# Splitting the first 8 MB load of a streaming ReLU-sum into a 2 MB and a 6 MB load

## The chip, the core and the metric

The kernel runs on one core of one Trainium2 chip. The metric is the device time of one execution in microseconds (us). The core has four engines that matter here: VectorE (DVE), ScalarE (ACT), GpSimd (POOL) and SyncE (SP), whose queue issues every DMA of this kernel; TensorE (PE) runs only a few matrix products whose result nobody reads. Sixteen DMA engines carry the data between the main memory (HBM) and the on-chip memory (SBUF), which has 128 partitions.

## The reference

The input `x` is 32 x 512 x 1024 float32, which is 16,384 rows of 1024 numbers, 67.1 MB. For each row the kernel clamps at zero and adds up:

```
relu_x = np.maximum(x, 0)
return np.sum(relu_x, axis=-1).astype(np.float32)
```

The output is 32 x 512 float32, 64 KB. So every byte of the input is read once, one maximum and one addition are done on each number, and almost nothing is written.

## The kernel before

**Tiling.** With 128 partitions there are NT = 128 rows for each partition. Rows are counted per partition by `m`, from 0 to 127, and `ROWS` = 16 of them make one full load: 128 partitions x 16 rows x 4 KB = 8 MB. Three SBUF buffers (`NBUF` = 3, called `io`) of that size are used in turn. The loads are:

- `j` = 0 to 6, the loop over `TWO`, `ACT` and `DVE`: seven full loads of 8 MB.
- then `TAIL`: one load of 8 rows a partition (4 MB) and one of 4 rows (2 MB), and the last 4 rows in four smaller loads of 1151, 436.5, 259 and 201.5 KB.

That is 13 loads. All are issued by SP through `load` (L104), in this order, on one queue, and each has a semaphore of its own.

**Where the rows lie.** The first 8 MB of the input (`xf`, L84) are one contiguous stretch: partition p holds 16 consecutive rows, so that the stretches of neighbouring partitions are 64 KB apart. The remaining 56 MB (`xv`, L85) are cut the same way with 112 rows a partition, so that there the pitch is 448 KB, and each full load takes 64 KB out of each. The functions `rows` and `sums` give the source of a load and the target of a store for a row number `m`.

**What is done to a load.** For each number n in `TWO[j]`, ACT clamps n rows a partition in one instruction (`clamp`, L145) and then DVE adds each row up in one instruction (`total`, L153), which waits for that ACT instruction. Load 0 and load 1 are one such piece of 16 rows, loads 2 to 4 two pieces of 8, load 5 two pieces of 7 and two rows that ACT does alone (`act_row`, L160), and load 6 is done row by row, 8 by ACT and 8 by DVE (`dve_row`, L168). The very first ACT instruction is the loading of the ReLU table (L143), and it waits for load 0.

**What sets the order around the change.** Load j, for j of 3 and up, goes into the buffer of load j - 3, so its issue on SP waits on the DVE semaphore until DVE has finished with that buffer (`freed[j - NBUF]`). Loads 0, 1 and 2 wait for nothing. `open_without_barrier` moves the first load alone (`EARLY` = 1) ahead of the program's opening. The stores come behind all loads in SP's order: the sums of the first 16 rows (`store(0, ROWS, ...)`, 8 KB, 64 bytes a partition), then 110 rows (55 KB), then the last two (1 KB), which waits for the last instructions of ACT and DVE. At the end SP waits until all stores have landed (L52).

Of the kernel before, what the change touches and what calls it, by code (L numbers as in the profile page):

```python
# [7 lines left out]
P = 128  # L8

ROWS = 16  # L10
NBUF = 3


TWO = [[16], [16], [8, 8], [8, 8], [8, 8], [7, 7], []]
ACT = [0, 0, 0, 0, 0, 2, 8]
DVE = [0, 0, 0, 0, 0, 0, 8]

# [2 lines left out]
TAIL = [8, 4]  # L20
# [11 lines left out]
def kernel(tc: tile.TileContext, x: bass.AP, out: bass.AP):  # L32
    nc = tc.nc
    sems = Semaphores(tc)

    tc.close()
    tc.compile()
    nc.cur_bb = nc.bb_map[tc.start_bb_name]
    body = nc.cur_bb.bb.instructions
    ends = list(body)  # L40
    body.clear()
    n_stores = relu_sum(nc, sems, x, out)
    body.extend(ends)


    nc.cur_bb = nc.bb_map[tc.start_bb_name + "_end"]
    nc.cur_bb.bb.instructions.clear()
    nums = sorted(s.num for s in (*sems.loads, sems.act, sems.dve))
    cleared = range(nums[0], nums[-1] + 1)
    assert len(cleared) == len(nums)  # L50
    nc.sync.sem_clear(cleared)
    nc.sync.wait_ge(sems.stored, 16 * n_stores).then_inc(sems.stored, -16 * n_stores)  # L52
    open_without_barrier(tc, EARLY)


class Semaphores:
    def __init__(self, tc: tile.TileContext):
        n = len(TWO) + len(TAIL) + 4
        self.loads = [tc.alloc_semaphore(f"load{i}") for i in range(n)]
        self.act = tc.alloc_semaphore("act")  # L60
        self.dve = tc.alloc_semaphore("dve")
        self.end = self.loads[-1]
        self.stored = tc.alloc_semaphore("stored")


def relu_sum(nc, sems: Semaphores, x: bass.AP, out: bass.AP):
    x_flat = x.flatten_outer_dims()
    N, D = x_flat.shape
    NT = N // P
    NB = len(TWO)  # L70
    assert N == P * NT == P * ROWS * (NB + 1)
    assert sum(TAIL) == ROWS - 4
    assert HEAD + MIDDLE + LAST_DVE == D and HEAD == 2 + LAST_DVE

    bufs = [nc.alloc_sbuf_tensor(f"io{i}", [P, ROWS, D], F32) for i in range(NBUF)]
    res = nc.alloc_sbuf_tensor("res", [P, NT], F32)
# [3 lines left out]
    last = nc.alloc_sbuf_tensor("last", [P, 2 + n_last + 2], F32)  # L80


    N1 = P * ROWS
    xf = x_flat[:N1].rearrange("(p m) d -> p m d", p=P)  # L84
    xv = x_flat[N1:].rearrange("(p m) d -> p m d", p=P)  # L85
    o_flat = out.rearrange("b s -> (b s)")
    of = o_flat[:N1].rearrange("(p m) -> p m", p=P)
    ov = o_flat[N1:].rearrange("(p m) -> p m", p=P)

    def rows(m, n):  # L90
        if m < ROWS:
            return xf[:, m : m + n, :]
        return xv[:, m - ROWS : m - ROWS + n, :]

    def sums(m, n):
        if m < ROWS:
            return of[:, m : m + n], res[:, m : m + n]
        return ov[:, m - ROWS : m - ROWS + n], res[:, m : m + n]

    n_load = n_act = n_dve = n_store = 0  # L100

    def load(dst, src, after=None):
        nonlocal n_load
        dma = nc.sync.dma_start(out=dst, in_=src)  # L104
        if after:
            dma.wait_op(sems.dve, after[1], "sem-ge")
        dma.then_inc(sems.loads[n_load], 16)
        n_load += 1
        return sems.loads[n_load - 1]

    def store(m, n, act, sem, count):
        nonlocal n_store
        dst, src = sums(m, n)
        if act:
            nc.sync.wait_ge(sems.act, act)
        nc.sync.dma_start(out=dst, in_=src).wait_op(sem, count, "sem-ge").then_inc(
            sems.stored, 16
        )
        n_store += 1
# [20 lines left out]
    def clamp(ap, loaded):  # L140
        nonlocal n_act
        if n_act == 0:
            nc.scalar.preload_act_table(RELU).wait_op(loaded, 16, "sem-ge")  # L143
            loaded = None
        i = nc.scalar.activation(out=ap, in_=ap, func=RELU)  # L145
        if loaded is not None:
            i.wait_op(loaded, 16, "sem-ge")
        i.then_inc(sems.act, 1)
        n_act += 1

    def total(ap, m, n):
        nonlocal n_dve
        nc.vector.tensor_reduce(  # L153
            out=res[:, m : m + n], in_=ap, axis=mybir.AxisListType.X, op=ADD
        ).wait_op(sems.act, n_act, "sem-ge").then_inc(sems.dve, 1)
        n_dve += 1

    def act_row(ap, accum_out, loaded):
        nonlocal n_act
        i = nc.scalar.activation(out=ap, in_=ap, func=RELU, accum_out=accum_out)  # L160
        if loaded is not None:
            i.wait_op(loaded, 16, "sem-ge")
        i.then_inc(sems.act, 1)
        n_act += 1

    def dve_row(ap, accum_out, loaded):
        nonlocal n_dve
        i = nc.vector.tensor_scalar(  # L168
            out=ap,
            in0=ap,  # L170
            scalar1=0.0,
            scalar2=None,
            op0=MAX,
            op1=ADD,
            accum_out=accum_out,
        )
        if loaded is not None:
            i.wait_op(loaded, 16, "sem-ge")
        i.then_inc(sems.dve, 1)
        n_dve += 1  # L180

    def multiply(done):
        ps = nc.alloc_psum_tensor("ps", [P, MM_COLS], F32)
        rows_of = bufs[(NB - 2) % NBUF]
        for k in range(N_MM):
            i = nc.tensor.matmul(  # L186
                ps[:, :], rows_of[:, 0, :P], rows_of[:, 1, :MM_COLS], start=True, stop=True
            )
            if k == 0:
                i.wait_op(sems.dve, done, "sem-ge").then_inc(sems.end, 1)  # L190

    freed = []
    m = 0
    for j in range(NB):
        buf = bufs[j % NBUF]
        loaded = load(buf[:, :, :], rows(m, ROWS), j >= NBUF and freed[j - NBUF])
        c = 0
        act_waits = dve_waits = loaded
        for n in TWO[j]:
            clamp(buf[:, c : c + n, :], act_waits)  # L200
            total(buf[:, c : c + n, :], m + c, n)
            act_waits = None
            c += n
        for _ in range(ACT[j]):
            act_row(buf[:, c, :], res[:, m + c : m + c + 1], act_waits)
            act_waits = None
            c += 1
        for _ in range(DVE[j]):
            dve_row(buf[:, c, :], res[:, m + c : m + c + 1], dve_waits)
            dve_waits = None  # L210
            c += 1
        assert c == ROWS
        freed.append((n_act, n_dve))
        m += ROWS


    multiply(freed[-1][1])
    buf = bufs[NB % NBUF]
    c = 0
    for n in TAIL:  # L220
        loaded = load(
            buf[:, c : c + n, :], rows(m, n), None if c else freed[NB - NBUF]
        )
        for i in range(n):
            if i % 2 == 0 or (n == 8 and i == 7):
                act_row(buf[:, c, :], res[:, m : m + 1], loaded if i == 0 else None)
            else:
                dve_row(buf[:, c, :], res[:, m : m + 1], loaded if i == 1 else None)
            c += 1
            m += 1  # L230

    flat = buf[:, :, :].rearrange("p c d -> p (c d)")
    src = rows(m, 4).rearrange("p c d -> p (c d)")
    at = c * D
    head = 2 * D + HEAD
# [4 lines left out]
    loaded = load(flat[:, at : at + head], src[:, :head])  # L240
# [8 lines left out]
    for lo, hi, n, first, second in (  # L249
# [3 lines left out]
        loaded = load(flat[:, at + lo : at + hi], src[:, lo:hi])  # L253
        act_part(flat[:, at + lo : at + lo + n], last[:, first : first + 1], (loaded, 16))
        dve_part(flat[:, at + lo + n : at + hi], last[:, second : second + 1], (loaded, 16))
    loaded = load(last[:, 2 : 2 + n_last], src[:, middle:end])
# [1 line left out]

    store(0, ROWS, freed[0][0], sems.dve, freed[0][1])
    store(ROWS, NT - ROWS - 2, sums_act, sems.dve, sums_dve)


# [62 lines left out]
```

## Time and profile before

| what | value |
|---|---|
| three timed runs | 160.92, 160.82 and 160.94 us, median 160.92 |
| span of the profiled execution, first to last instruction | 159.9 us |
| what lies around the span, if the profiled execution took the median time | about 1.0 us |
| data read | 67.11 MB, 420 GB/s over the span |
| DVE busy | 118.7 us (74%) |
| ACT busy | 103.6 us (65%) |
| PE busy | 8.6 us |
| load 0 issued, first consumer starts | 0.00 us, 22.27 us |
| last store issued, landed | 158.51 us, 1.4 us later |

The profile gives the profiled execution's span, and no time of its own besides; the third row is the difference of the median and the span. The page counts an engine as busy only while it works on an instruction. DMA queues are told in packets: one packet is what one DMA engine moves in one piece, here the stretch of one partition. In the views that follow, "idle before, releaser" is the time an engine stood still ahead of an instruction and the thing whose end let it go on; `SPq` is SyncE's queue, which issues DMAs and is otherwise idle.

### The profile page before, as it was taken

The numbers are of one execution on the slowest core, as the hardware profiler recorded it, in microseconds if no ns is written. First come the engines' busy times: TensorE is split into PE (matmuls) and PEld (weight loads), VectorE is DVE, ScalarE is ACT, GpSimd is POOL, SyncE is SP. The second block draws the span as 40 slices with busy tenths as digits, with TensorE's granted clock in tenths as the row PEclk, the third lists the DMA queues.
The fourth block names the chain that finished last, engine by engine and source line by source line (L and its number), as shares of the span: only waits on it lengthen the run. The fifth ranks groups of instructions, "written<-read, shape, count | busy, mean of one in ns | idle before, by whom it ended". The sixth has DMA issues, their size and how long they took to land.

```text
span 159.9 us, 157 instructions
## 1 busy us (share of the span) xinstructions
PE 8.6 (5%) x16; PEld 3.6 (2%) x16; DVE 118.7 (74%) x44; ACT 103.6 (65%) x53; POOL 1.0 (1%) x5
## 2 busy tenths in 40 slices
PE   0000000000000000000000000000000000000695
PEld 0000000000000000000000000000000000000241
DVE  0000000006999799999999999999999799999986
ACT  0000049993599807997099950999429993397995
POOL 0000000000000000000000000000000000000001
DMA  8996996996996997999979979969969969899993
GB/s 279 508 492 295 524 492 295 524 492 295 525 492 295 524 475 311 524 393 393 525 328 459 508 344 459 508 295 508 492 295 524 492 295 524 377 402 402 428 396 110
DMA packets 2304, 67.18 MB, mean 420 GB/s; under 512 B 640, under 2 KB 768, under 8 KB 1024
## 3 DMA queue, kind: packets, MB, share of 16 engines
q1 hardware_dynamic: 2304, 67.18, 97.8%
HBM read 67.11 MB, written 0.07 MB: 420 GB/s over the span
## 4 chain that ended last, share of the span: by engine, by line
DMA 45%; DVE 45%; ACT 9%; SPq 1%; issue 0%
DMA io<-in_x_dram 45%; DVE res L153 43%; ACT io L145 9%; DVE io L168 1%; SPq L104 1%; DVE io L127 1%; DVE io L266 0%
## 5 line engine op out<-in xcount | busy, mean ns | idle before, releaser
L153 DVE TENSOR_REDUCE res<-io 128x8 f32<-128x8192 f32 (+2 forms) x10 | 101.1, 10173 | 39.2 <-ACT io L145 39.2
L145 ACT ACTIVATE io<-io 128x8192 f32<-128x8192 f32 (+2 forms) x10 | 81.8, 8218 | 25.9 <-DMA io<-in_x_dram 25.9
L160 ACT ACTIVATE io<-io 128x1024 f32<-128x1024 f32 x18 | 18.8, 1042 | 6.6 <-DMA io<-in_x_dram 6.6
L186 PE MATMUL ps<-io 128*128 128x512 f32 x16 | 8.6, 698 | 149.5 <-DVE io L168 149.5
L168 DVE TENSOR_SCALAR_CACHE_REDUCE io<-io 128x1024 f32<-128x1024 f32 x14 | 16.2, 1215 | 0.5 <-DMA io<-in_x_dram 0.4
L143 ACT ACT_TABLE_LOAD x1 | 1.3, 1283 | 22.3 <-DMA io<-in_x_dram 22.3
L186 PEld LDWEIGHTS ps<-io 128*128 128x128 f32 x16 | 3.6, 231 | 153.7 <-DVE io L168 149.5
L160 ACT ACTIVATION_READ_ACCUMULATOR io<-io 128x1 f32 x18 | 3.3, 186 | 0.0
L246 POOL TENSOR_SCALAR io<-io 128x254 f32<-128x254 f32 x1 | 0.8, 841 | 155.4 <-DMA io<-in_x_dram 155.4
L168 DVE DVE_READ_ACCUMULATOR io<-io 128x1 f32 x14 | 1.2, 82 | 0.0
L127 DVE TENSOR_SCALAR_CACHE_REDUCE io<-io 128x552 f32<-128x552 f32 (+1 forms) x2 | 1.1, 594 | 0.0
L122 ACT ACTIVATE io<-io 128x321 f32<-128x321 f32 (+1 forms) x2 | 0.9, 426 | 0.1
L266 DVE SCALAR_TENSOR_TENSOR io<-last,io 128x254 f32<-128x254 f32 x1 | 0.4, 423 | 0.0
L122 ACT ACTIVATION_READ_ACCUMULATOR io<-io 128x1 f32 x2 | 0.4, 186 | 0.0
L122 ACT ACTIVATE last<-last 128x153 f32<-128x153 f32 x1 | 0.3, 330 | 0.0
L122 ACT ACTIVATION_READ_ACCUMULATOR last<-last 128x1 f32 x1 | 0.2, 187 | 0.0
L127 DVE DVE_READ_ACCUMULATOR io<-io 128x1 f32 x2 | 0.2, 82 | 0.0
L311 POOL MEMSET const-uint8-127<- 128x1 uint8 x1 | 0.1, 102 | 0.0
L311 POOL MEMSET const-bfloat16-1.0<- 128x1 bf16 x1 | 0.1, 101 | 0.0
L311 POOL MEMSET const-float32-0.0<- 128x1 f32 x1 | 0.1, 99 | 0.2 <-issue 0.2
L311 POOL MEMSET const-float32-1.0<- 128x1 f32 x1 | 0.1, 98 | 0.0
L266 DVE DVE_READ_ACCUMULATOR io<-last,io 128x1 f32 x1 | 0.1, 82 | 0.0
## 6 DMA issues: line engine op xcount, KB each, us to landing
io<-in_x_dram SPq DMA_DIRECT2D x1, 4096.0 KB, 23.7
io<-in_x_dram SPq DMA_DIRECT2D x1, 2048.0 KB, 28.3
io<-in_x_dram SPq DMA_DIRECT2D x1, 1151.0 KB, 30.6
io<-in_x_dram SPq DMA_DIRECT2D x1, 436.5 KB, 31.2
io<-in_x_dram SPq DMA_DIRECT2D x1, 259.0 KB, 31.4
last<-in_x_dram SPq DMA_DIRECT2D x1, 201.5 KB, 31.4
io<-in_x_dram SPq DMA_DIRECT2D x7, 29.0
out_dram<-res SPq DMA_DIRECT2D x1, 55.0 KB, 1.6
```

The source lines that it names most:

```text
L104: dma = nc.sync.dma_start(out=dst, in_=src)
L122: nc.scalar.activation(out=ap, in_=ap, func=RELU, accum_out=accum_out).wait_op(*after, "sem-ge").then_inc(sems.end, 1)
L127: i = nc.vector.tensor_scalar(out=ap, in0=ap, scalar1=0.0, scalar2=None, op0=MAX, op1=ADD, accum_out=accum_out,)
L143: nc.scalar.preload_act_table(RELU).wait_op(loaded, 16, "sem-ge")
L145: i = nc.scalar.activation(out=ap, in_=ap, func=RELU)
L153: nc.vector.tensor_reduce(out=res[:, m : m + n], in_=ap, axis=mybir.AxisListType.X, op=ADD).wait_op(sems.act, n_act, "sem-ge").then_inc(se ...
L160: i = nc.scalar.activation(out=ap, in_=ap, func=RELU, accum_out=accum_out)
L168: i = nc.vector.tensor_scalar(out=ap, in0=ap, scalar1=0.0, scalar2=None, op0=MAX, op1=ADD, accum_out=accum_out,)
L186: i = nc.tensor.matmul(ps[:, :], rows_of[:, 0, :P], rows_of[:, 1, :MM_COLS], start=True, stop=True)
L246: nc.gpsimd.tensor_scalar(out=clamped, in0=clamped, scalar1=0.0, scalar2=None, op0=MAX).wait_op(loaded, 16, "sem-ge").then_inc(sems.end, 1)
L266: nc.vector.scalar_tensor_tensor(out=clamped, in0=last[:, : 2 + LAST_DVE], scalar=0.0, in1=clamped, op0=MAX, op1=ADD, accum_out=res[:, NT ...
L311: nc = _bacc.Bacc("TRN2", target_bir_lowering=False, num_devices=1)
```

## The change

The first 8 MB are no longer one contiguous stretch cut into 128 pieces of 16 rows. They become two stretches. The first 2 MB hold 4 rows a partition (`FIRST` = 4; stretches 16 KB apart), the next 6 MB hold 12 rows a partition (48 KB apart). Each is loaded by a DMA of its own into its part of the same buffer, so there are 14 loads. `EARLY` stays 1, so the 2 MB load alone is moved ahead of the opening. ACT and DVE take this buffer in a piece of 4 rows and a piece of 12 rows; the ACT instruction of each piece waits for its own load (the table load for the first). Load 3 waits for both pieces as it did for the one. The sums of these rows leave in two stores, of 16 and 48 bytes a partition, where there was one of 64. All other rows keep their places, loads and instructions.

```diff
-TWO = [[16], [16], [8, 8], [8, 8], [8, 8], [7, 7], []]
+FIRST = 4
+TWO = [[FIRST, ROWS - FIRST], [16], [8, 8], [8, 8], [8, 8], [7, 7], []]
...
-        n = len(TWO) + len(TAIL) + 4
+        n = len(TWO) + len(TAIL) + 5
...
-    N1 = P * ROWS
-    xf = x_flat[:N1].rearrange("(p m) d -> p m d", p=P)
-    xv = x_flat[N1:].rearrange("(p m) d -> p m d", p=P)
...
+    parts = []
+    for lo, hi in ((0, FIRST), (FIRST, ROWS), (ROWS, NT)):
+        src = x_flat[P * lo : P * hi].rearrange("(p m) d -> p m d", p=P)
+        dst = o_flat[P * lo : P * hi].rearrange("(p m) -> p m", p=P)
+        parts.append((lo, hi, src, dst))
...
-        loaded = load(buf[:, :, :], rows(m, ROWS), j >= NBUF and freed[j - NBUF])
+        if j == 0:
+            loads = [
+                load(buf[:, lo:hi, :], rows(lo, hi - lo)) for lo, hi, _, _ in parts[:2]
+            ]
+        else:
+            loads = [
+                load(buf[:, :, :], rows(m, ROWS), j >= NBUF and freed[j - NBUF])
+            ]
         c = 0
-        act_waits = dve_waits = loaded
-        for n in TWO[j]:
+        act_waits = dve_waits = loads[0]
+        for k, n in enumerate(TWO[j]):
+            if k and k < len(loads):
+                act_waits = loads[k]
             clamp(buf[:, c : c + n, :], act_waits)
             total(buf[:, c : c + n, :], m + c, n)
...
-    store(0, ROWS, freed[0][0], sems.dve, freed[0][1])
+    store(0, FIRST, freed[0][0], sems.dve, freed[0][1])
+    store(FIRST, ROWS - FIRST, 0, sems.dve, freed[0][1])
     store(ROWS, NT - ROWS - 2, sums_act, sems.dve, sums_dve)
```

More of the change, by code (lines that the diff above doesn't have):

```diff
@@ L80, in relu_sum, with part_of @@
     last = nc.alloc_sbuf_tensor("last", [P, 2 + n_last + 2], F32)
-    N1 = P * ROWS
-    xf = x_flat[:N1].rearrange("(p m) d -> p m d", p=P)
-    xv = x_flat[N1:].rearrange("(p m) d -> p m d", p=P)
     o_flat = out.rearrange("b s -> (b s)")
-    of = o_flat[:N1].rearrange("(p m) -> p m", p=P)
-    ov = o_flat[N1:].rearrange("(p m) -> p m", p=P)
+    parts = []
[3 more added lines that the diff above has]
+        parts.append((lo, hi, src, dst))
+    def part_of(m, n):
+        return next(p for p in parts if p[0] <= m and m + n <= p[1])
     def rows(m, n):
-        if m < ROWS:
-            return xf[:, m : m + n, :]
-        return xv[:, m - ROWS : m - ROWS + n, :]
+        lo, _, src, _ = part_of(m, n)
+        return src[:, m - lo : m - lo + n, :]
     def sums(m, n):
-        if m < ROWS:
-            return of[:, m : m + n], res[:, m : m + n]
-        return ov[:, m - ROWS : m - ROWS + n], res[:, m : m + n]
+        lo, _, _, dst = part_of(m, n)
+        return dst[:, m - lo : m - lo + n], res[:, m : m + n]
     n_load = n_act = n_dve = n_store = 0
```

## The prediction

> **What bounds the kernel now.** I read the page's slices and queue first, then the table of stretches cut at the arrivals of the loads, then the order of instructions, and last the waits of SP's queue against the chain. The page:
>
> ```profile
> span 159.9 us, 157 instructions
> ...
> DMA  8996996996996997999979979969969969899993
> ...
> q1 hardware_dynamic: 2304, 67.18, 97.8%
> HBM read 67.11 MB, written 0.07 MB: 420 GB/s over the span
> ## 4 chain that ended last, share of the span: by engine, by line
> DMA 45%; DVE 45%; ACT 9%; SPq 1%; issue 0%
> ```
>
> The queue's packets fill 97.8% of what sixteen engines have to give in the span. The chain at the bottom looks different: it gives DVE as much as the DMA. Which is right is decided by the arrivals. Stretches cut where ACT gets each full load (columns: stretch and length, busy time of the engines, TensorE clock, DMA share, GB/s):
>
> ```profile
> 22.30:41.60 19.30, 0.00 (x0) 0.00 (x0) 4.15 (x1) 15.11 (x3) 0.00 (x0) 1.00 1.00 435
> 41.60:60.95 19.35, 0.00 (x0) 0.00 (x0) 18.53 (x2) 13.86 (x2) 0.00 (x0) 1.00 1.00 434
> 60.95:80.30 19.35, 0.00 (x0) 0.00 (x0) 19.35 (x2) 13.96 (x3) 0.00 (x0) 1.00 1.00 434
> 99.65:119.00 19.35, 0.00 (x0) 0.00 (x0) 19.35 (x3) 13.96 (x3) 0.00 (x0) 1.00 1.00 434
> ```
>
> Every 8 MB takes the same 19.35 us with a DMA share of 1.00, whether DVE was busy for 4 us of it or for all of it. Had a load waited for a free buffer, its arrival would be late; none is. The order of work around the first buffer:
>
> ```profile
> 22.27 1.28 ACT L143 ACT_TABLE_LOAD   x1 [22.27 <-DMA io<-in_x_dram]
> 23.56 13.86 ACT L145 ACTIVATE io<-io 128x16384 f32<-128x16384 f32 x1
> 37.45 17.22 DVE L153 TENSOR_REDUCE res<-io 128x16 f32<-128x16384 f32 x1 [37.45 <-ACT io L145]
> 41.60 13.86 ACT L145 ACTIVATE io<-io 128x16384 f32<-128x16384 f32 x1 [4.18 <-DMA io<-in_x_dram]
> 54.70 0.33 SPq L104 DMA_DIRECT2D io<-in_x_dram  x1
> 55.49 17.22 DVE L153 TENSOR_REDUCE res<-io 128x16 f32<-128x16384 f32 x1 [0.82 <-ACT io L145]
> 60.95 7.03 ACT L145 ACTIVATE io<-io 128x8192 f32<-128x8192 f32 x1 [5.49 <-DMA io<-in_x_dram]
> ```
>
> DVE frees buffer 0 and SP issues load 3 at 54.70, but load 2 keeps the DMA engines until 60.95: the issue is 6.25 us early. SP's later issues, at 72.73, 89.92, 107.11 and 124.29, precede the arrivals at 80.29, 99.65, 118.99 and 138.35 of the loads ahead of them by 7 to 14 us. So this wait of the queue, large as it is, costs nothing:
>
> ```profile
> SPq L104 <- DVE res L153: 121.6, 5, 53.3
> ```
>
> The kernel is bound by the DMA stream from its first packet to its last, plus a beginning and an end in which the stream does not run. The beginning and the end:
>
> ```profile
> 0.00:0.90 0.90, 0.00 (x0) 0.00 (x0) 0.00 (x0) 0.00 (x0) 0.19 (x4) 1.00 0.00 0
> 1.60:1.90 0.30, 0.00 (x0) 0.00 (x0) 0.00 (x0) 0.00 (x0) 0.00 (x0) 1.00 1.33 437
> ...
> 157.60:157.80 0.20, 0.20 (x2) 0.00 (x0) 0.20 (x3) 0.20 (x1) 0.00 (x0) 1.00 0.02 2
> 158.20:158.40 0.20, 0.00 (x0) 0.00 (x0) 0.20 (x2) 0.20 (x2) 0.00 (x0) 1.00 0.00 0
> 158.40:159.20 0.80, 0.00 (x0) 0.00 (x0) 0.08 (x2) 0.07 (x1) 0.00 (x0) 1.00 0.00 0
> ```
>
> A packet counts in the stretch in which it starts. No packet starts in the first 0.90 us, and the last of the sixteen engines starts only between 1.60 and 1.90. At the end DMA is idle around 157.7 and from 158.2 to 159.2, before the last store.
>
> **The change, part by part.** The sum is made on the profiled execution: span 159.94 us, and about 0.98 around it to the median of 160.92 (the runs lie within 0.12 of each other). I call the change visible from 0.2%, that is 0.32 us: below 160.60 or above 161.24.
>
> *Two loads for one, in the stream.* The trace's packet records give, per packet and engine, 2.418 us for 64 KB, 1.213 for 32 KB and 0.611 for 16 KB (the later full loads, the 4 MB and the 2 MB load). Doubling the size adds 0.602 for 16 KB and 1.205 for 32 KB, so 16 KB cost 0.602 and each packet 0.009 besides; 48 KB is then 1.815. Each engine serves 8 partitions: before 8 x 2.418 = 19.344, after 8 x (0.611 + 1.815) = 19.408, so +0.064, and a completion packet of 0.009 more: +0.073 on the path, because nothing in the stream hides it. The timeline agrees: ACT gets load 6 at 138.35 and the 4 MB load at 148.06, 9.71 after, against half of 19.35 = 9.68; a load more in a full queue costs a few hundredths.
>
> The Trainium skill, page "SBUF — State Buffer", section "The DMA setup-cost knee", speaks against this change: every transfer pays roughly 2 us that do not scale with its bytes, so one should coalesce into the largest single transfer. Were that paid in series, the sum would be 160.92 + 2.0 = 162.9 as an estimate from that page; the 9.71 above shows no such term for a load that is queued behind another, so the trace contradicts it there, and shows it only at the beginning of the stream.
>
> *The seam.* The 6 MB load has to be queued when the 2 MB load runs out. SP issued its first three loads at 0.00, 0.43 and 0.91, and the first packet started 1.01 after the first issue. Issued at 0.43, the 6 MB load is ready at about 1.5 to 2.3 (the last engine's start was 0.83 behind the first's). The 2 MB load ends 8 x 0.611 = 4.89 after the engines' start and their first delay, at 5.9 at the earliest. Cover: over 3.5 us. Cost taken: 0; if the cover were gone, up to 1.4, the time from issue to landing of the lone last store.
>
> *The start.* The first packets take 2.63 to 3.38 us in the records where the later ones take 2.42, and the engines start over 0.83 us. As all move the same bytes afterwards, they keep this order: sixteen completions of load 0 arrive from 21.27 to 22.25, fourteen by 21.75 and the two last at 22.12 and 22.25; the same tail is in every later load up to the end. So the slowest engine's start sets the end of the kernel. The change alters the first addresses and the size of the first packet (16 KB), and no row shows that. From below: if the two late engines joined the other fourteen, 0.50 is won. From above: a further delay of the same 0.50. The delay looks like a latency, which 16 KB pay as 64 KB do, and the pitch of 448 KB of later loads runs at the full rate as 64 KB does, so I take 0.
>
> *Instructions of ACT and DVE.* The table load and the first clamp move forward: the 2 MB load lands at 22.27 - (19.344 - 4.888) = 7.8 instead of 22.27. ACT: 1.28 + 4/16 x 13.86 = 4.7, to 12.5; DVE 4/16 x 17.22 = 4.3, to 16.9. The 12 rows land at 22.35: ACT 10.4 to 32.8, DVE 12.9 to 45.7. The two extra instructions cost ACT and DVE some tenths at most, in the 4.18 us that ACT idles ahead of 41.60. Load 3 can be issued at 45.7 instead of 54.70, but DMA engines have loads 1 and 2 until 61: hidden, 0. From load 1 on (ACT at 41.60 + 0.07, DVE behind it) nothing moves but by the 0.07.
>
> *Issues on SP.* One load more, 0.43 us, past which loads 1 and 2 move from 0.43 and 0.91 to 0.9 and 1.4; they are needed at 22 and 41. One store more at 127.2, about 0.37; behind it SP next waits for ACT until 156.9, so it is hidden.
>
> *The stores in the ring.* The 8 KB store is issued at 127.21 and lands 31.0 us later, since it queues behind the loads. Its packets (64 B, 0.011 us) become twice as many (16 and 48 B; the 8 B packets of the last store take 0.007 to 0.009), which adds 8 x 0.010 + 0.009 = 0.09 per engine, after the last load, in the hole at 157.7. If the hole is too small, the 55 KB store shifts by under 0.1, and behind it stands the idle time of 1.0 ahead of the last store's packets. Nothing on the path: 0.
>
> Sum: +0.064 + 0.009 = +0.073: the span becomes 160.0, and the time 160.92 + 0.07 = 161.0.
>
> **The rivals.**
> - *The late engines start better.* The two late ones lose part of their 0.50: 160.6 to 160.9, and at the full amount 161.0 - 0.50 = 160.5. For it: a first packet of 16 KB keeps sixteen engines closer together in memory. Against it: nothing shows that addresses set the delay.
> - *The late engines start worse*, by the same 0.25 to 0.50: 161.25 to 161.5. For it: a third and fourth load are issued while the engines start. Against it: that was so with three.
> - *The seam opens* (the slower side): the 6 MB load's packets come after the 2 MB load ran out, or the engines restart there. Price up to 1.4, so 161.3 to 162.4; it decides from a gap of 0.25 us. Against it: 3.5 us of cover, and the seams of the tail show 0.03. For it: those seams had full queues for 20 us, this one lies in the first 6 us.
> - *Earlier work pays* (the chain is right and the DMA waits for DVE): load 3 is released 9.0 us earlier, and up to that much is won: 152. Against it: the steps of 19.35 at share 1.00.
>
> **How the numbers follow.** Forecast as summed, 0.63. Late engines better 0.16, of which 0.11 passes below 160.60. Late engines worse 0.09, of which 0.07 passes above 161.24. Seam 0.10. Earlier work 0.02. Faster 0.11 + 0.02 = 0.13; slower 0.07 + 0.10 = 0.17; same 0.70. The range reaches down to the late engines' whole gain, 160.55 when rounded, and up to most of their loss and a small seam, 161.4; left out are the large seam, the earlier work and the edges, under 2 in 10.
>
> **What would show it.** The table load should start at 7.8 and the 12-row clamp at 22.3 to 22.4; ACT's next arrivals at 41.67, 61.0, 80.4, each 0.07 later than before, at steps of 19.35. Load 3's issue should be at 45.7 with no effect on 80.4. If the first arrivals after the seam are off by more than 0.2 from this, start or seam is wrong: with the table load on time and the 12-row clamp late it is the seam, with both shifted alike it is the start. A last store that lands more than 1.5 us after its issue would speak for the stores. DMA share under 0.99 between 22.3 and 138.4 would overthrow the bound itself.

## The result, and the profile after

The changed kernel took 161.63 us (five runs, 161.52 to 161.70) where the kernel before took 160.92 (160.81 to 161.15): a ratio of 1.0040 with a 95% interval from 1.0027 to 1.0052. It is 0.71 us slower. The forecast was 161.0, no visible change, with a range up to 161.4; the time lies outside.

The page of the changed kernel, in the lines that answer to those of before:

```profile
span 160.1 us, 161 instructions
...
DMA  7999998998989979979969969969969979898994
...
q1 hardware_dynamic: 2592, 67.18, 98.0%
HBM read 67.11 MB, written 0.07 MB: 420 GB/s over the span
## 4 chain that ended last, share of the span: by engine, by line
DMA 44%; DVE 37%; ACT 13%; PE 6%; SPq 1%; issue 0%
```

The span is 160.1 us where it was 159.9, with 288 packets more: two DMAs of 128 packets and 16 completions each. These two spans give at most 0.2 us of the 0.71. The chain now names PE because the matrix products that nobody reads ran until 159.20; the last store was issued at 158.65, before they ended, so they hold nothing up. The stretches between arrivals of full loads (same columns as before the change):

```profile
22.30:41.70 19.40, 0.00 (x0) 0.00 (x0) 8.90 (x1) 10.45 (x2) 0.00 (x0) 1.00 1.00 432
61.05:80.40 19.35, 0.00 (x0) 0.00 (x0) 19.35 (x2) 13.96 (x3) 0.00 (x0) 1.00 1.00 434
```

From 22.3 us on the stream runs as before, 8 MB in 19.35 us at a DMA share of 1.00. The order of work around the first buffer:

```profile
7.82 1.28 ACT L145 ACT_TABLE_LOAD   x1 [7.82 <-DMA io<-in_x_dram]
9.11 3.62 ACT L147 ACTIVATE io<-io 128x4096 f32<-128x4096 f32 x1
12.76 4.42 DVE L155 TENSOR_REDUCE res<-io 128x4 f32<-128x4096 f32 x1 [12.76 <-ACT io L147]
...
22.33 10.44 ACT L147 ACTIVATE io<-io 128x12288 f32<-128x12288 f32 x1 [9.60 <-DMA io<-in_x_dram]
32.80 12.95 DVE L155 TENSOR_REDUCE res<-io 128x12 f32<-128x12288 f32 x1 [15.62 <-ACT io L147]
41.69 13.86 ACT L147 ACTIVATE io<-io 128x16384 f32<-128x16384 f32 x1 [8.92 <-DMA io<-in_x_dram]
45.78 0.33 SPq L106 DMA_DIRECT2D io<-in_x_dram  x1
```

ACT begins 14.5 us earlier and SP issues load 3 at 45.78 instead of 54.70, and neither moves the arrivals: load 1 reaches ACT at 41.69, a little later than the 41.60 of the profile before. That wait of SP's queue is still large in the list of waits and still costs nothing:

```profile
SPq L106 <- DVE res L155: 120.9, 5, 43.6
```

The stores, from issue to landing in us (the last column):

```profile
out_dram<-res SPq DMA_DIRECT2D x1, 55.0 KB, 2.4
out_dram<-res SPq DMA_DIRECT2D x1, 2.0 KB, 30.7
out_dram<-res SPq DMA_DIRECT2D x1, 6.0 KB, 30.8
out_dram<-res SPq DMA_DIRECT2D x1, 1.0 KB, 1.4
```

The 55 KB store lands 2.4 us after its issue where it took 1.6; the last one takes 1.4 as before.

The two profiles thus agree with the forecast nearly everywhere and differ by 0.2 us, and the measured times differ by 0.71. So the first question was what the profile of before stood for.

### The profile page after: what moved, and what is told of

It reads as the page before. It is cut to its first block, busy times and chain, and to the rows that moved or that the text cites. A ratio compares the mean times of both kernels' runs of the same rounds, so it can differ in the third digit from the quotient of the medians.

```text
span 160.1 us, 161 instructions
## 1 busy us (share of the span) xinstructions
PE 9.6 (6%) x16; PEld 3.9 (2%) x16; DVE 118.9 (74%) x45; ACT 103.7 (65%) x54; POOL 1.0 (1%) x5
## 4 chain that ended last, share of the span: by engine, by line
DMA 44%; DVE 37%; ACT 13%; PE 6%; SPq 1%; issue 0%
DMA io<-in_x_dram 44%; DVE res L155 31%; ACT io L147 13%; PE ps L188 6%; DVE io L170 6%; SPq L106 1%
## 5 line engine op out<-in xcount | busy, mean ns | idle before, releaser
L155 DVE TENSOR_REDUCE res<-io 128x8 f32<-128x8192 f32 (+4 forms) x11 | 101.3, 9261 | 39.1 <-ACT io L147 39.1
L147 ACT ACTIVATE io<-io 128x8192 f32<-128x8192 f32 (+4 forms) x11 | 82.0, 7489 | 40.2 <-DMA io<-in_x_dram 40.2
L188 PE MATMUL ps<-io 128*128 128x512 f32 x16 | 9.6, 766 | 149.6 <-DVE io L170 149.6
```

The lines of the kernel that those rows point to most:

```text
L155: nc.vector.tensor_reduce(out=res[:, m : m + n], in_=ap, axis=mybir.AxisListType.X, op=ADD).wait_op(sems.act, n_act, "sem-ge").then_inc(se ...
L188: i = nc.tensor.matmul(ps[:, :], rows_of[:, 0, :P], rows_of[:, 1, :MM_COLS], start=True, stop=True)
```

## The experiments

Times are compared by their ratio to runs of the kernel before on the same chip. "Arrival" is the time at which ACT gets load 1 in the profiled execution of each kernel, that is, when the second 8 MB are there; from there up to the stores all kernels go on alike, so it shows how late the start of that one execution was. Executions of one kernel differ in it: with the first load's source untouched the arrivals below run from 41.08 to 41.58. "Outside" is an execution's time less its span, as the median over the kernel's executions (spans are on record to 0.1 us).

| kernel | median us | ratio to before, 95% interval | arrival | outside |
|---|---|---|---|---|
| changed kernel | 161.63 | 1.0040 (1.0027 to 1.0052) | 41.69 | 1.52 |
| before, again | 161.03 | 1.0007 (0.9998 to 1.0015) | 41.31 | 1.33 |
| load alone split | 161.01 | 1.0009 (0.9998 to 1.0020) | 41.08 | 1.51 |
| store alone split | 161.05 | 1.0009 (1.0000 to 1.0018) | 41.58 | 1.33 |
| one semaphore more | 161.02 | 1.0004 (0.9995 to 1.0013) | 41.24 | 1.33 |
| pieces alone split | 161.13 | 1.0016 (1.0007 to 1.0024) | 41.48 | 1.52 |
| 12 rows first | 161.92 | 1.0058 (1.0045 to 1.0070) | 41.89 | 1.52 |
| 8 rows first | 161.28 | 1.0016 (1.0007 to 1.0025) | 41.15 | 1.48 |
| 5 rows first | 161.78 | 1.0053 (1.0040 to 1.0067) | 41.82 | 1.48 |
| 2 rows first | 163.16 | 1.0136 (1.0117 to 1.0154) | 41.12 | 1.58 |
| load split, 16 KB pitch | 161.59 | 1.0037 (1.0025 to 1.0049) | 41.58 | 1.53 |
| load split, 48 KB pitch | 161.60 | 1.0038 (1.0026 to 1.0051) | 41.67 | 1.53 |
| load split, 32 KB pitch | 161.13 | 1.0006 (0.9997 to 1.0015) | 41.26 | 1.51 |
| load split, 80 KB pitch | 161.10 | 1.0007 (0.9998 to 1.0015) | 41.10 | 1.54 |
| load split, 96 KB pitch | 160.99 | 0.9999 (0.9987 to 1.0010) | 40.98 | 1.50 |
| load split, 448 KB pitch | 161.16 | 1.0012 (1.0003 to 1.0021) | 41.36 | 1.46 |
| changed, 64 KB pitch in load 0 | 161.14 | 1.0013 (1.0005 to 1.0022) | 41.12 | 1.52 |
| before, 16 KB pitch | 161.33 | 1.0023 (1.0015 to 1.0032) | 41.61 | 1.33 |
| before, loads 0 and 1 exchanged | 160.98 | 0.9999 (0.9990 to 1.0008) | 41.33 | 1.36 |

"Pitch" is the distance of neighbouring partitions' stretches in the source of the first load alone. The load-split kernels have both loads, the two pieces and one store; the last two kernels work the first buffer in one piece. The same kernel against itself (second row) gives 1.0007, so a tenth of a percent is as fine as the ratios go.

**One part at a time.** Theory: the split load, the split store, the longer program or the extra semaphore costs the 0.7. First, the load alone in two, at the old addresses (with its semaphore, and with the two pieces of work that follow from it):

```diff
-TWO = [[16], [16], ...
+TWO = [[4, 12], [16], ...
-        n = len(TWO) + len(TAIL) + 4
+        n = len(TWO) + len(TAIL) + 5
...
+            loads = [
+                load(buf[:, lo:hi, :], rows(lo, hi - lo)) for lo, hi in ((0, 4), (4, 16))
+            ]
```

> The load alone is split: 4 and 12 rows of the one 8 MB stretch (64 KB apart as before), two pieces of work, one more semaphore, one store of 64 bytes a partition as before. Theory of the load (an extra DMA and its seam in the first microseconds cost 0.7 us): 161.5 to 161.7. Theory of the stores (the two stores of 16 and 48 bytes cost 0.6): 161.0, that is 0.07 to 0.1 over before, with a span of 160.0 and about 1.0 around it. Theory of the program (one more semaphore, more instructions): 161.5 or so, with 1.5 around the span.

It took 161.01, ratio 1.0009. The store alone:

```diff
-    store(0, ROWS, freed[0][0], sems.dve, freed[0][1])
+    store(0, 4, freed[0][0], sems.dve, freed[0][1])
+    store(4, ROWS - 4, 0, sems.dve, freed[0][1])
```

> The store alone is split: the first 16 sums leave in stores of 16 and 48 bytes a partition, 64 bytes apart; one load of 8 MB as before. Theory of the stores: 161.5, most of it around the span. Theory of the load: 160.9 to 161.0. Theory of the program (one instruction more, no semaphore more): 160.9 if the semaphore is what costs.

161.05, ratio 1.0009. One semaphore more:

```diff
+        self.spare = tc.alloc_semaphore("spare")
...
-    nums = sorted(s.num for s in (*sems.loads, sems.act, sems.dve))
+    nums = sorted(s.num for s in (*sems.loads, sems.spare, sems.act, sems.dve))
```

> One more semaphore is reserved and cleared at the end, and nothing else is changed. Theory of the program: up to 161.5. Theories of the load and of the stores: 160.92, no change.

161.02, ratio 1.0004. The pieces alone:

```diff
-TWO = [[16], [16], ...
+TWO = [[4, 12], [16], ...
```

> The first buffer is clamped and added up in pieces of 4 and 12 rows behind the one load of 8 MB; one more instruction on ACT and one on DVE, no DMA more. Theory of the program by its length: above 161.2. All other theories: 160.92, no change, since the pieces lie in the idle time of ACT ahead of load 1.

161.13, ratio 1.0016. None of the four is the 0.7; each is 0.1 to 0.2% or less. But the 0.24 us of the pieces is clear of the scatter, and the last column shows where it lies: their spans are those of the kernel before (median 159.6 in both), and 1.52 us lie outside the span instead of 1.33. This parts all the kernels here into two groups. In each of the 179 executions with the first buffer in one piece on record, time less span is 1.28 to 1.41; in each of the 117 with two pieces it is 1.43 to 1.62. So one more instruction on ACT and one on DVE cost about 0.2 us that no view of the profile shows; one more semaphore, or one more store, costs none there. Which of the two instructions it is, and why, stays open.

What none of the four has is the new layout of the source. In the profiled executions the kernel with two loads at the old addresses gets load 1 at 41.08 and the changed kernel 0.61 later, though the same bytes came in two loads in both. A single arrival does not prove this: of the eleven executions of the former, seven took 160.86 to 161.01 with spans of 159.4 or 159.5, and four took 161.36 to 161.49 with spans of 159.9. None of the four was profiled, so it is not shown that they lost their 0.5 us at the start; but arrivals do reach 41.58 at the old addresses, in the kernel with the store alone split. So a late start seems to occur there too, now and then.

**Other splits of the same 8 MB.** One constant of the changed kernel:

```diff
-FIRST = 4
+FIRST = 12   # and 8, 5, 2
```

> The changed kernel with its two stretches the other way round: first 6 MB with 48 KB between partitions, then 2 MB with 16 KB. Theory of the close start (with 16 KB between partitions the first packets of the sixteen engines hinder each other, and the slowest engine starts 0.6 us later for good): the 16 KB stretch is now met in mid-stream and costs nothing, 161.0 to 161.1. Theory of the sum (load, stores, semaphore and pieces each cost a little over 0.1 and add up, wherever the stretches lie): 161.5 to 161.6 as in the changed kernel.

> The changed kernel with two stretches of 4 MB, 32 KB between partitions. Theory of the close start: between the cases, 161.1 to 161.4, with first packets that are late by about half as much. Theory of the sum: 161.5 to 161.6.

> The changed kernel with a first stretch of 2.5 MB, 20 KB between partitions, which is no power of two. If the close start is a matter of a small stretch alone: nearly as 4 rows, 161.4 to 161.6. If it is a matter of addresses that repeat at powers of two: 161.0 to 161.1. Theory of the sum: 161.5 to 161.6.

> The changed kernel with a first stretch of 1 MB, 8 KB between partitions. Theory of the close start: at least as slow as 4 rows, 161.6 to 162.2, with first packets that are later still. Theory of the sum: 161.5 to 161.6.

12 rows first was to be fast by the theory of a close start, and is slow, 161.92, with the latest arrival of all. 8 rows first is nearly free (161.28), 5 rows slow (161.78). So neither a plain sum of the parts nor nearness alone holds, and the pitch of the first load, 48, 32 or 20 KB here, may be what matters, not in order of size; packets and stores change with it in these kernels. Two rows first is slowest, 163.16, but its arrival is early, 41.12: its time is lost elsewhere. Its stores show where (issue to landing in the last column; the third row stands for the two stores of 1 KB, one of them the last of the kernel):

```profile
out_dram<-res SPq DMA_DIRECT2D x1, 55.0 KB, 3.4
out_dram<-res SPq DMA_DIRECT2D x1, 7.0 KB, 31.6
out_dram<-res SPq DMA_DIRECT2D x2, 1.0 KB, 17.0
```

The 55 KB store takes 3.4 us instead of 1.6, and by the completion records the last store, issued at 158.16, is complete only at 161.18, 3.0 us later instead of 1.4. Its data packets are done by 159.18, so it is the completion that is late. This is a second effect, of the stores: behind stores of 8 and 56 bytes a partition later stores complete late. In the kernel with 8 rows first, stores of 32 bytes leave the 55 KB store at 1.6. Size alone does not settle it. The kernel with the store alone split sends the same 16 and 48 bytes a partition as the changed kernel, but 64 bytes apart in the output where the changed kernel packs each store closely, and its 55 KB store takes 1.8 against 2.4:

```profile
out_dram<-res SPq DMA_DIRECT2D x1, 55.0 KB, 1.8
out_dram<-res SPq DMA_DIRECT2D x1, 2.0 KB, 30.5
out_dram<-res SPq DMA_DIRECT2D x1, 6.0 KB, 30.7
```

No run here parts size from spacing.

**The first load's addresses alone.** To part the first load's addresses from all else, the kernel with the load alone split gets only another source for its 2 MB:

```diff
-                load(buf[:, lo:hi, :], rows(lo, hi - lo)) for lo, hi in ((0, 4), (4, 16))
+                load(buf[:, :4, :], x_flat[: P * 4].rearrange("(p m) d -> p m d", p=P)),
+                load(buf[:, 4:, :], rows(4, 12)),
```

> As the kernel with the load alone split (two loads of 4 and 12 rows, one store, measured at 161.0), but the source of the 2 MB load alone is changed to the first 2 MB, 16 KB between partitions; the 6 MB load still comes with 64 KB between partitions, so some rows are summed twice and others not at all, and the sums of the first four rows of a partition are those of other rows. Theory of the close start (the first load's addresses make the slowest engine start late): 161.5 to 161.7, the load after the first 8 MB lands 0.4 to 0.6 us later. Theory of the stores' layout or of the 6 MB load's layout: 161.0.

And the reverse, the changed kernel with the old addresses in its first load alone:

```diff
+                    x_flat[: P * ROWS].rearrange("(p m) d -> p m d", p=P)[:, :FIRST, :],
...
+                load(buf[:, FIRST:, :], rows(FIRST, ROWS - FIRST)),
```

> The changed kernel, but its 2 MB load alone comes with 64 KB between partitions (wrong rows for the first four sums of a partition); the 6 MB load with 48 KB and the two stores of 16 and 48 bytes stay as changed. Theory of the close start: back to 161.0 to 161.1. Theory of the stores or of the 6 MB load's layout: 161.6 as in the changed kernel.

Both came out as the first load's addresses would have it: 161.59 with them in a kernel that has nothing else of the new layout, 161.14 without them in a kernel that has all the rest. The order of ACT's work, first with the 16 KB pitch, then the changed kernel with 64 KB:

```profile
7.69 1.28 ACT L143 ACT_TABLE_LOAD   x1 [7.69 <-DMA io<-in_x_dram]
...
41.58 13.86 ACT L145 ACTIVATE io<-io 128x16384 f32<-128x16384 f32 x1 [8.91 <-DMA io<-in_x_dram]
```

```profile
7.24 1.28 ACT L145 ACT_TABLE_LOAD   x1 [7.24 <-DMA io<-in_x_dram]
...
41.12 13.86 ACT L147 ACTIVATE io<-io 128x16384 f32<-128x16384 f32 x1 [8.91 <-DMA io<-in_x_dram]
```

Each belongs beside its own partner. The kernel with the load alone split has these rows at 7.19 and 41.08: the 16 KB pitch makes both 0.50 later. The changed kernel has them at 7.82 and 41.69: 64 KB pitch makes both some 0.57 earlier. So the delay is there in the first load and is carried unchanged to the next. The packet records place it: the sixteen engines' first packets of 16 KB, 0.611 us each in mid-stream, took 0.96 to 1.43 us in the changed kernel with 64 KB pitch and 0.71 to 1.96 in the changed kernel as it is; most later packets of the same load are at 0.611 again, and the 6 MB load's are all at 1.815. First packets are not all: the packets that end this load last in the changed kernel, at 7.45 us, follow one another without a pause from one of 1.11 us that began at 2.09, after all sixteen engines had started. The late engine then stays late. All five executions with the 16 KB pitch took 161.43 to 161.67, and only four of the eleven with 64 KB came near that (161.36 to 161.49): the pitch makes regular what otherwise seems to occur now and then.

The same in the kernel before, without any split:

```diff
+        if j == 0:
+            src = bass.AP(tensor=src.tensor, offset=src.offset, ap=[[4 * D, P], [D, ROWS], [1, D]])
```

> The kernel before with one load of 8 MB, whose source alone is changed: 64 KB a partition, but only 16 KB between the partitions' beginnings, so that the reads overlap and the first 16 sums of most partitions are those of other rows. No split, one store. Theory of the close start: 161.4 or more, since the first packets are as close as in the changed kernel. If the start suffers only in small packets or in a split load: 160.9 to 161.0.

161.33, ratio 1.0023: slower than before with no split and no new store, by 0.37 us, so packets of 64 KB suffer too. It is less than the 161.4 expected. With its one piece this kernel has 1.33 us outside the span; its span, 160.0, is that of the load-split kernel with 16 KB pitch, which has 1.53 outside. Here the reads of neighbouring partitions also overlap, which no run parts from the pitch.

**The kernel before, once more.**

> The kernel before, once more, for its span beside the time of the same execution. If what lies around the span is 1.4 to 1.6 as in the other kernels, the execution first profiled (span 159.94) took about 161.4 and was a slow one of its kind; if it is 1.0, the changed kernel spends 0.5 us outside of its span.

This execution had a span of 159.7 and took 161.0: 1.3 us lie around the span, as in every execution of this kernel whose span is on record (1.28 to 1.41; the changed kernel: 161.63 and 160.1, so 1.5). With 1.28 to 1.41 around its 159.94, the execution that the forecast was built on took about 161.2 to 161.35, above every run of 160.81 to 161.15 shown beside it. So the about 1.0 us around the span in the table of before is too small, and the spans that go with the two median times, about 159.6 and 160.1, differ by 0.5 and not by 0.2. The arrivals here say the same:

```profile
21.99 1.28 ACT L143 ACT_TABLE_LOAD   x1 [21.99 <-DMA io<-in_x_dram]
...
41.31 13.86 ACT L145 ACTIVATE io<-io 128x16384 f32<-128x16384 f32 x1 [4.17 <-DMA io<-in_x_dram]
```

Here load 0 arrives at 21.99 and load 1 at 41.31, where they were at 22.27 and 41.60. The kernel is the same; between these two executions the start differs by 0.3 us.

**Which pitches.** Five more kernels ask what it is in the addresses, all with `P * 4` replaced in the source of the 2 MB load:

```diff
-                load(buf[:, :4, :], x_flat[: P * 4].rearrange("(p m) d -> p m d", p=P)),
+                load(buf[:, :4, :], x_flat[: P * 12].rearrange("(p m) d -> p m d", p=P)[:, :4, :]),
```

> The kernel with the load alone split, its 2 MB load alone with 48 KB between partitions (the rows summed first are partly other rows than the reference's). If any nearness of the first addresses costs in proportion: between the 161.59 of 16 KB and the 161.01 of 64 KB, nearer to the latter, 161.1 to 161.25. If it is the pitch of 48 KB itself that made the kernel with 6 MB first slow: 161.4 to 161.9. If that slowness lay in the seam in mid-stream: 161.0.

> The same with 32 KB between partitions in the 2 MB load alone (partly other rows). Nearness in proportion: 161.25 to 161.45. If pitches of larger powers of two are free: 161.0 to 161.1.

> The same with 448 KB between partitions in the 2 MB load alone, as the later loads have it (partly other rows). Nearness: 161.0 or up to 0.1 less. If only multiples of 64 KB are free: 161.0 too. If a power of two is needed: 161.3 or more.

> The kernel with the load alone split, its 2 MB load alone with 96 KB between partitions, three times 32 KB (the rows summed first are partly other rows than the reference's). If every multiple of 32 KB starts well: 161.0 to 161.2, the load after the first 8 MB reaches ACT at 41.1 to 41.35. If the pitch must be a multiple of 64 KB or a power of two: 161.5 to 161.7, and 41.55 to 41.7.

> The same with 80 KB between partitions, five times 16 KB and farther apart than the 64 KB that started well. If an odd multiple of 16 KB starts badly however far apart: 161.5 to 161.7. If distance is what helps: 161.0 to 161.2.

48 KB is as slow as 16 KB (161.60, arrival 41.67), 32 KB is fast (161.13, 41.26), and so are 80, 96 and 448 KB; only one of the eleven executions at 96 KB took 161.72. The theory of nearness falls with 48 KB, slower than 32. The theory that a multiple of 32 KB is needed, formed on these, falls with 80 KB. What is shown is a list, not a rule: in this kernel, first loads of 16 KB a partition at 16 and 48 KB pitch are some 0.45 us slow in all five executions of each, at 32, 64, 80, 96 and 448 KB in some or none. Why stays open.

**A version that beats both?** The exchange of the first two loads, with the wide pitch first:

```diff
+        m = (ROWS, 0)[j] if j < 2 else j * ROWS
...
-    store(0, ROWS, freed[0][0], sems.dve, freed[0][1])
+    store(0, ROWS, freed[1][0], sems.dve, freed[1][1])
```

> The kernel before with its first two loads exchanged: load 0 takes 16 rows a partition with 448 KB between partitions, load 1 the contiguous 8 MB; nothing split, all sums right. If the start is cheaper the farther the first addresses lie apart: 160.7 to 160.9, a version that beats both. If 64 KB is already free: 160.95, no change.

160.98 against 160.98: no change. 64 KB was already free, and no version here beats the kernel before.

## Why the prediction was wrong, point by point

- *The bound* was right. Steps of 19.35 us before and after; the chain that gave DVE 45% was no limit, and the rival by which 9 us of earlier release would pay is refuted: load 3 was issued at 45.78 instead of 54.70 and arrived at 80.38 instead of 80.29. The sign "share under 0.99 between 22.3 and 138.4" was badly chosen, since the kernel before itself falls under it in a stretch that the prediction did not show:

```profile
119.00:138.35 19.35, 0.00 (x0) 0.00 (x0) 18.42 (x3) 14.31 (x7) 0.00 (x0) 1.00 0.96 413
```

  This is a matter of counting: the step is 19.35 like the others and the packet records show no pause in it, but a packet counts where it starts, and the packets of the next load, which begin within the stretch, are shorter.
- *Two loads for one, +0.073*: right within what can be seen. From the table load to the 12-row clamp the changed kernel took 22.33 - 7.82 = 14.51, against 8 x 1.815 + 0.009 = 14.53. Split at the old addresses, the load costs 0.1 at most in the median (161.01 against 160.89), the two pieces included. The 2 us for each transfer that the Trainium skill states (page "SBUF — State Buffer", section "The DMA setup-cost knee") are not paid by a load queued behind another, as these runs show again.
- *The seam* was right: the 6 MB load's packets follow without a gap.
- *The start, taken as 0*, is the main step that failed. The text named the slowest engine's start as what sets the end, gave bounds of 0.50 either way, and chose 0 because the delay "looks like a latency, which 16 KB pay as 64 KB do", and because a pitch of 448 KB runs at the full rate in mid-stream. Packet size was indeed not what mattered. The addresses were, and the rate in mid-stream said nothing of them: 161.59 against 161.01 in otherwise equal kernels, 161.63 against 161.14 in the reverse pair, about 0.45 us by the ratios. The rival "the late engines start worse" had this mechanism and this size with a chance of 0.09. Its argument, a third and fourth load issued during the start, was not the reason: the fast split kernels issue four loads too.
- *The sum's base* was wrong as well, though the forecast time, a median plus 0.073, does not hang on it. "About 0.98 around" the span mixed the span of one execution with the median of others. What lies around is 1.3 in the kernel before and 1.5 in the changed one, and the execution shown was late by about 0.3 in its start. So the arrivals forecast from it (7.8, 22.35, 41.67; measured 7.82, 22.33, 41.69) agree to 0.02 by luck: a late start of the kernel before was extended to the changed one, which starts late regularly. For the same reason the signs named for a wrong start, arrivals off by more than 0.2, did not show although the start was wrong.
- *The stores* were right for the end, but "shifts by under 0.1" was not: the 55 KB store landed 2.4 us after its issue instead of 1.6, though its packets came as soon after the issue as before. It was complete about 0.5 us ahead of the last store, so most of the cover had gone. With 64 KB pitch in the first load and the same stores it took 2.8, and the last one 1.5 instead of 1.4.
- *Instructions of ACT and DVE*, taken as hidden in ACT's idle time, is the second step that failed. Inside the span they are hidden. Outside it the two extra instructions cost 0.2 us: the kernel that has them and nothing else took 161.13, with 1.52 outside the span instead of 1.33. No row that the prediction read could show this.
- *The issues on SP*: right, hidden.

Of the 0.71 us, some 0.45 are shown to be the first load's addresses and about 0.2 the two pieces, outside the span. With the 0.07 that the prediction added for the extra load this makes 0.7; the 0.07 us itself is smaller than the 0.1 us by which the kernel differs from itself (ratio 1.0007) and is not parted from it.

## What to carry to other kernels

When a stream of transfers bounds a kernel from its first packet on, what delays one DMA engine in its first packets is paid in full at the end, and the layout of the first transfer deserves a trial of its own, whatever its rate later. Starting the compute engines earlier is worth nothing where they were already waiting for data, and here the extra instructions for it were not free. And a forecast of tenths of a microsecond must not add one execution's span to another's time: take span and time of the same execution, compare spans with spans, and know how far executions of the same kernel differ.

## What was unexpected in the hardware

- The pitch of the first load's source changes the start of the stream by about 0.45 us (16 and 48 KB slow in every execution; 32, 64, 80, 96 and 448 KB in some executions or none), with no effect on the rate afterwards.
- One more instruction on ACT and one on DVE add about 0.2 us outside the span from first to last instruction (1.51 against 1.33 in the median), where the profile shows nothing.
- Small stores can delay the completion of other stores behind them: with 8 and 56 bytes a partition the 55 KB store took 3.4 us and the last store 3.0 instead of 1.6 and 1.4; with 16 and 48 bytes 2.4 for the first of these when each store is packed and 1.8 when its pieces lie 64 bytes apart; with 32 and 32 bytes 1.6, nothing. What in them does it is not shown.
